# A two-layer hybrid trunk on one core: attention exponentials turned by VectorE and transfers, mixer transfers moved to GpSimd's queue, and fewer small matmuls for norms

## The chip, the cores and the metric

The kernel runs on one core of one Trainium2 chip. The core has five engines with an instruction queue each: TensorE (PE in the profile; PEld is its weight load), VectorE (DVE), ScalarE (ACT), GpSimd (POOL) and SyncE (SP). SP, ACT and POOL can also issue transfers, which 16 DMA engines carry out. The metric is device time in microseconds of one launch, lower is better.

## The reference, cut to what matters

One sequence of 256 tokens with 2048 features goes through two layers; each layer is a mixer and then a gated feed-forward block with a short convolution, all with a norm ahead and a residual around. Everything is float32.

```python
h = rms_norm(x, mix_norm[0])                       # layer 0, mixer A/B
u, v, q, f, i, g = split(h @ w_in)                 # 6 blocks of 1024 columns
u, v = gelu(u), gelu(v)
v = rms_norm(v per head)                           # A: 8 heads of 128
y_a = u * (causal_w @ v + b)                       # chunks of 128 tokens
log_f = logaddexp(log(lb), log1p(-lb) + log_sigmoid(f)); k = (1 - lb) * sigmoid(-f)
o = gated linear recurrence of q, k, i, log_f      # B: 8 heads of 128, linear in q
y_b = rms_norm(o per head, gain) * silu(g)
x = x + concat(y_a, y_b) @ w_out
x = x + conv_ffn(rms_norm(x, ffn_norm[0]))
h = rms_norm(x, mix_norm[1])                       # layer 1, mixer C
q, k, v, g, f = split(h @ w_in); q, k = rms_norm(q), rms_norm(k)   # 16 heads of 128
c = cumsum(log_sigmoid(f + b_f))                   # one number per head and token
p = softmax(causal(q @ k.T * scale + c[t] - c[s]))
x = x + ((p @ v) * sigmoid(g)) @ w_out
x = x + conv_ffn(rms_norm(x, ffn_norm[1]))
```

## The kernel before, in words

**Weights.** Every projection streams its weights from HBM in chunks of 512 KB (L181, on SP's queue). ScalarE rounds a chunk to the matmul's format (`wh`, L175) and VectorE takes the rest (`wl`, L176); activations are split the same way. A product is then three matmuls (activation high times `wh`, high times `wl`, low times `wh`), each 128x128 by 512, at L292 to L294 (`project_tok`) and L311 to L313 (`project_four`). A chunk gives twelve of these. `w` has four buffers, `wh` and `wl` three.

**Steps.** All other work is written as generators. Each chunk begins with a `tick()`: every generator in flight (at most `depth[0]`) runs to its next `yield`, and its instructions thus stand in the program ahead of that chunk's. `LAG`, `WAIT`, `PACE` are counts of such steps. A scheduler then orders each engine's instructions by priority (the order of the program) and readiness; `held(r, "wh")` or `held(r, "wl")` says that an instruction may not come ahead of the last weight half written so far, and `tied` does that for matmuls.

**Turning.** Projections give tokens on partitions where features are wanted. `transposed` does this in two moves: `blocks` (L324) transposes 32x32 blocks on VectorE, and `moves` (L331) sends 16 transfers of 32 KB from tile to tile, dealt out to SP and POOL in turn. `add_four` (L462 to L474) does it for the residual after an output projection; half of its transfers go out a step later for two of the four quarters.

**Norms.** `Norm` adds up squares of x in `acc`. `finish_tok` (L434) sums over partitions with matmuls two columns wide and gives `Rt`, the reciprocal root with tokens on partitions; `finish` (L445) sums with a 128x128 matrix of ones and gives `R`, with tokens along the row on every partition. `rsq` (L389 to L394) is the reciprocal root: a multiply-add, logarithm and exponential on ScalarE, and three VectorE operations.

**Mixer A/B.** `q` of each head is taken from PSUM by `fold` (L337, L338) and multiplied by `R` (L802, L803). `hgrn(h)` is the recurrence of one head: a small product (L681) for the diagonal, seven levels of halving with VectorE and ScalarE, small matmuls (L721), and the output (L743 to L745) in a bank of PSUM, of which there are two. ScalarE squares it there (L749), `rsq` follows, and two scaled copies (L753) write it out. `gated(j)` multiplies four heads with silu of the gate, turns them and splits them into `yb`; `spatial(j)` does the A half and gives `ya`. `values` needs `Rt` with its second half of tokens reversed, `Rr`, made by a matmul with a reversed identity (L594). The output projection (`stretch`) takes `yb` first, then `ya`.

**Mixer C.** `forget` computes the 16 forget logits with x itself (L901), so `sums` multiplies by `R`, makes the running sum `fc` and sends it through DRAM (`cd`, L928) to all partitions (`cb`, L934), on POOL's queue. The q, k, v columns come in four groups of four heads, 24 chunks a group; q and k are normed by head and turned. `attend(h)` runs for two heads at a time during the next group's chunks: scores (L954, L955), bias and mask (L958 to L962, reading `cb`), maximum (L968), exponentials, three transposes of 128x128 on TensorE (L977), a copy out of PSUM (L980), the product with v (L984 to L986) and a scaled copy (L988). `gate(q)` multiplies with sigmoid of the gate once all heads are done, turns, and splits for the output projection.

Of the kernel before, what the change touches and what calls it, by code (L numbers as in the profile page):

```python
# [15 lines left out]
P = 128  # L16
S = 256
# [9 lines left out]
FORGET = 4  # L27
WAIT = 4
# [25 lines left out]
def tile_trunk(ctx: ExitStack, tc: tile.TileContext, x, pp_d, cst_d, mlev_d, msk_d,  # L54
# [262 lines left out]
    def transposed(src, tmp, dst, queues=(nc.sync, nc.gpsimd)):  # L317

        blocks(src, tmp)
        moves(tmp, dst, queues)  # L320
# [6 lines left out]
    def moves(tmp, dst, queues=(nc.sync, nc.gpsimd), rows=range(4)):  # L327
        n = 2 * BLK
        for a in rows:
# [4 lines left out]

    def fold(ps):
        t = tp.tile([P, S], F32, tag="ev", name=nm("ev"), bufs=3)
        SC.activation(t, ps[:, S:2 * S], AF.Copy)  # L337
        V.tensor_tensor(t, ps[:, 0:S], t, ALU.add)  # L338
        return t

    def project_norm(wsrc, acts, R, out=None, run=2):
        t = fold(project(wsrc, acts, run=run))
        if out is None:
            out = t
        V.tensor_tensor(out, t, R, ALU.mult)
        return out
# [53 lines left out]
    class Norm:  # L400
# [42 lines left out]
        def finish(self, tok=False):  # L443
            ps = bank()
            PE.matmul(ps[:, 0:S], ones, self.acc, start=True, stop=True)  # L445
            R = cp.tile([P, S], F32, tag="R", name=nm("R"), bufs=2)
            rsq(R, ps[:, 0:S], D)
            if not tok:
                return R
            for _ in self.finish_tok():  # L450
                pass
            return R, self.Rt

# [6 lines left out]
    def add_four(q, ps, z, tmp, dst, nxt, halves=1):  # L460
# [25 lines left out]
    def mixer_ab(norm):  # L486
# [11 lines left out]
        gv, late = [], []  # L498

        def finish():  # L500
            for k in range(KT):
                norm.feed_square(k)
                if k % 2:
                    yield
            late.extend(norm.finish(tok=True))

        for g, ps in enumerate(project_first(w_v, norm, lambda: queue.append(finish()))):
# [5 lines left out]
            else:  # L513
                drain()
                R, Rt = late
# [77 lines left out]
        ps = bank()  # L593
        PE.matmul(ps[:, 0:2], cst[:, K_REV:K_REV + P], Rt, start=True, stop=True)  # L594
        Rr = hp.tile([P, LANE], F32, tag="Rr", name="Rr")[:, 0:2]
        V.tensor_copy(Rr[:, 0:1], Rt[:, 0:1])
        V.tensor_copy(Rr[:, 1:2], ps[:, 1:2])
# [21 lines left out]

        queue.append(mixes())  # L620
        lf, kq = [], []

        def gates(j, z):

            for _ in range(LAG):
                yield
# [15 lines left out]
        for j in range(2):  # L642
# [5 lines left out]
            transposed(lambda T: z[:, T * 512:(T + 1) * 512], tmp, t.rearrange("p (m t) -> p m t", m=4))  # L648
# [4 lines left out]
        itoks, left, os_ = [], [NH], []  # L653

# [12 lines left out]
        def hgrn(h):  # L667
# [78 lines left out]
            so = hp.tile([P, LANE], F32, tag="so", name=nm("so"), bufs=2)[:, 0:2]  # L746
            ot = hp.tile([P, P], F32, tag="ot", name=nm("ot"), bufs=1)
            for T in range(2):
                SC.activation(ot, op[:, T * P:(T + 1) * P], AF.Square,  # L749
                              accum_out=so[:, T:T + 1])  # L750
            rsq(so, so, P)
            for T in range(2):
                SC.activation(os_[h // 4][:, T, d0:d0 + P], op[:, T * P:(T + 1) * P], AF.Copy,  # L753
                              scale=so[:, T:T + 1])
# [13 lines left out]
        def gated(j):  # L768
# [17 lines left out]
            moves(tmp, t.rearrange("p (m t) -> p m t", m=4))  # L786
            for _ in range(LAG - 1):
                yield
# [5 lines left out]
        for h in range(NH):  # L794
# [16 lines left out]
        def spatial(j, z):  # L811
            for _ in range(LAG):
                yield
# [487 lines left out]
```

## Time and profile before

| what | value |
|---|---|
| runs | 2288.85, 2288.69, 2287.63 us; median 2288.69 |
| span of the profiled execution | 2287.3 us; the median of the runs is 1.4 us more, which is what lies around the span and the spread |
| granted TensorE clock | 1.000 |
| TensorE busy | 2280.8 us |
| VectorE, ScalarE, GpSimd busy | 1559.8, 1309.6, 361.2 us |
| mixer A/B, first feed-forward, mixer C, second feed-forward | about 0 to 407, 407 to 1126, 1126 to 1592, 1592 to 2287 us |

The page of the profile has busy times, the span in 40 slices, the DMA queues, the chain of work that ended last, the costliest groups and the DMA issues. A row of a timeline is: start, duration, engine, line, operation, output from input, shapes, count, and in brackets the idle time of the engine ahead of it and what ended it. A row of groups is: line, engine, operation, tiles, shapes, count, then busy time and mean ns of one, then idle time ahead of it. A row of waits is: who waited, for whom, total, times, longest. A row of one line's instructions gives the shortest, middle and longest duration in ns, and the first and last start. A row of windows gives the stretch, its length, then for each engine busy time and instructions, the granted clock, the DMA engines' share and GB/s.

### The profile page before, as it was taken

The numbers are of one execution on the slowest core, as the hardware profiler recorded it, in microseconds if no ns is written. First come the engines' busy times: TensorE is split into PE (matmuls) and PEld (weight loads), VectorE is DVE, ScalarE is ACT, GpSimd is POOL, SyncE is SP. The second block draws the span as 40 slices with busy tenths as digits, with TensorE's granted clock in tenths as the row PEclk, the third lists the DMA queues.
The fourth block names the chain that finished last, engine by engine and source line by source line (L and its number), as shares of the span: only waits on it lengthen the run. The fifth ranks groups of instructions, "written<-read, shape, count | busy, mean of one in ns | idle before, by whom it ended". The sixth has DMA issues, their size and how long they took to land.

```text
span 2287.3 us, 32261 instructions
## 1 busy us (share of the span) xinstructions
PE 2280.8 (100%) x10832; PEld 1893.5 (83%) x10832; DVE 1559.8 (68%) x2309; ACT 1309.6 (57%) x1980; POOL 361.2 (16%) x662
## 2 busy tenths in 40 slices
PE   9999999999999999999999999999999999999999
PEld 8888888888888888888888888888888888888887
DVE  7788767777467656766875675767776476657766
ACT  7677756666456445654565555655665465456642
POOL 0121221212012002111111111211211012012102
PEclk9999999999999999999999999999999999999999
DMA  8655767778667667776666655777777677667765
GB/s 288 195 169 160 215 199 235 238 216 234 193 208 221 206 201 213 220 213 186 213 227 203 194 177 181 220 224 242 225 217 218 195 216 210 209 205 216 223 204 174
DMA packets 489415, 480.45 MB, mean 210 GB/s; under 512 B 114112, under 2 KB 457168, under 8 KB 489120
## 3 DMA queue, kind: packets, MB, share of 16 engines
q1 hardware_dynamic: 467040, 453.54, 64.2%
q0 software_dynamic: 20480, 22.50, 4.3%
q10 hardware_dynamic: 1728, 2.35, 0.3%
q8 instruction: 85, 1.39, 0.3%
q14 instruction: 82, 0.67, 0.1%
HBM read 435.24 MB, written 2.11 MB: 191 GB/s over the span
## 4 chain that ended last, share of the span: by engine, by line
PE 97%; DVE 2%; ACT 1%; issue 0%; SPq 0%; DMA 0%; DVEq 0%; ACTq 0%
PE pm L311 26%; PE pm L312 26%; PE pm L313 26%; PE pm L292 4%; PE pm L294 4%; PE pm L293 4%; PE pm L193 1%; PE pm L266 1%; PE pm L217 1%; DVE wl L176 0%; PE pm L269 0%; ACT wh L175 0%; DVE kq L701 0%; PE px L955 0%; SPq L331 0%
## 5 line engine op out<-in xcount | busy, mean ns | idle before, releaser
L176 DVE TENSOR_TENSOR wl<-w,wh 128x1024 fp32r<-128x1024 f32 (+1 forms) x820 | 996.9, 1219 | 637.0 <-ACT wh L175 629.3
L175 ACT ACTIVATE wh<-w 128x1024 fp32r<-128x1024 f32 (+1 forms) x820 | 862.5, 1054 | 786.0 <-PE pm L313 552.3
L311 PE MATMUL pm<-wh,a 128*128 128x512 f32 x1728 | 674.4, 390 | 0.0
L312 PE MATMUL pm<-wl,a 128*128 128x512 f32 x1728 | 672.5, 389 | 0.0
L313 PE MATMUL pm<-wh,a 128*128 128x512 f32 x1728 | 672.5, 389 | 0.0
L331 POOL DMA_DIRECT2D zt<-tmp x413 | 223.5, 549 | 1201.6 <-DVE tmp L324 1089.8
L313 PEld LDWEIGHTS pm<-wh,a 128*128 128x128 f32 x1728 | 324.4, 188 | 67.4
L312 PEld LDWEIGHTS pm<-wl,a 128*128 128x128 f32 x1728 | 324.4, 188 | 67.3 <-DVE wl L176 0.5
L311 PEld LDWEIGHTS pm<-wh,a 128*128 128x128 f32 x1728 | 324.4, 188 | 67.1
L311 PE MATMUL pm<-wh,hid 128*128 128x512 f32 x688 | 267.6, 389 | 0.0
L312 PE MATMUL pm<-wl,hid 128*128 128x512 f32 x688 | 267.6, 389 | 0.0
L313 PE MATMUL pm<-wh,hid 128*128 128x512 f32 x688 | 267.6, 389 | 0.0
L331 POOL DMA_DIRECT2D turn<-tmp x160 | 86.7, 550 | 504.5 <-DVE tmp L324 256.7
L292 PE MATMUL pm<-wh,a 128*128 128x512 f32 x416 | 165.2, 397 | 0.0
L294 PE MATMUL pm<-wh,a 128*128 128x512 f32 x416 | 162.1, 390 | 0.0
L293 PE MATMUL pm<-wl,a 128*128 128x512 f32 x416 | 162.0, 389 | 0.0
L311 PEld LDWEIGHTS pm<-wh,hid 128*128 128x128 f32 x688 | 129.2, 188 | 26.9
L313 PEld LDWEIGHTS pm<-wh,hid 128*128 128x128 f32 x688 | 129.2, 188 | 26.8
L312 PEld LDWEIGHTS pm<-wl,hid 128*128 128x128 f32 x688 | 129.2, 188 | 26.7
L1105 ACT ACTIVATE conv<-zt,pp 128x256 f32<-128x256 f32 x176 | 95.9, 589 | 26.1 <-DMA zt<-tmp 22.2
L324 DVE STREAM_TRANSPOSE tmp<-z 128x512 f32<-128x512 f32 x120 | 83.4, 704 | 18.9 <-ACT z L1091 18.4
L294 PEld LDWEIGHTS pm<-wh,a 128*128 128x128 f32 x416 | 78.1, 188 | 16.6
(244 smaller groups left out, 2075.6 us busy)
## 6 DMA issues: line engine op xcount, KB each, us to landing
w<-in_w_up SPq DMA_DIRECT2D x352, 512.0 KB, 4.4
w<-in_w_dn SPq DMA_DIRECT2D x176, 512.0 KB, 4.5
w<-in_w_cqkv SPq DMA_DIRECT2D x96, 512.0 KB, 4.3
w<-in_w_abo SPq DMA_DIRECT2D x32, 512.0 KB, 4.6
w<-in_w_cg SPq DMA_DIRECT2D x32, 512.0 KB, 4.3
w<-in_w_co SPq DMA_DIRECT2D x32, 512.0 KB, 4.3
zt<-tmp SPq DMA_DIRECT2D x414, 32.0 KB, 2.7
zt<-tmp POOLq DMA_DIRECT2D x413, 32.0 KB, 2.5
```

The costliest lines, as they stand in the source:

```text
L175: r = deep["wh"] = SC.activation(wh, w, AF.Copy)
L176: deep["wl"] = V.tensor_tensor(wl, w, wh.bitcast(F32), ALU.subtract)
L193: PE.matmul(ps[g][T], a[:, o + T * P:o + (T + 1) * P], t[:, i * 512:(i + 1) * 512], start=k + i + j == 0, stop=k + i == KT - 1 and j == 2)
L292: PE.matmul(ps[T], ah, h, start=k + i == 0, stop=False)
L293: PE.matmul(ps[T], ah, l, start=False, stop=False)
L294: deep["last"] = PE.matmul(ps[T], al, h, start=False, stop=k + i == KT - 1)
L311: PE.matmul(ps[T], ah, h, start=not begun and k + i == ks[0], stop=False)
L312: PE.matmul(ps[T], ah, l, start=False, stop=False)
L313: deep["mm"] = deep["last"] = PE.matmul(ps[T], al, h, start=False, stop=not more and k + i == ks[-1] + 1)
L324: V.transpose(tmp.rearrange("p (b m i t) -> p b m i t", b=4, m=4, t=2)[:, :, :, :, T], src(T).rearrange("p (m b j) -> p b m j", m=4, b=4))
L331: queues[(a + b) % len(queues)].dma_start(dst[BLK * b:BLK * (b + 1), :, a * n:(a + 1) * n], tmp[BLK * a:BLK * (a + 1), b * 4 * n:(b + 1) * ...
L1105: held(SC.activation(c, z, AF.Identity, bias=pp[:, cb:cb + 1], scale=w(2)))
```

## The change

Six things change, none in the feed-forward blocks.

1. `attend` takes two heads at once. Exponentials of both lie in one tile of six 128x128 blocks; VectorE transposes their 32x32 blocks (two instructions of 128x384) and 16 transfers on POOL put the blocks in place. The transposes on TensorE and the copy out of PSUM go. The products stand six steps behind the last of the transfers' steps; a pair starts at least `PAIR` = 5 steps after the one ahead. While the gate's weights stream, three generators may be in flight.
2. All of the mixers' `moves` go to POOL alone (`ONE`), except the last set of each mixer's gate or residual (`TWO`); the readers' `LAG` grows by one step, and `add_four` no longer splits its transfers.
3. `hgrn` writes its output raw by one copy; squares are taken from the copy, scaled by `Rt`, and after every fourth head one `rsq` and two 128x512 products norm four heads. `q` is no longer multiplied by `R`: the recurrence is linear in q, so its norm is folded into the output's factor.
4. `finish` and its ones-by-`acc` matmul go from both mixers. `sums` gets its norm from four matmuls with 32 columns of ones, 64 tokens each, into four strips of 32 partitions.
5. `Rr` is made by VectorE transposes and copies in `mirror`.
6. `yB` in mixer C is filled by place.

```diff
+PAIR = 5
...
+    ONE, TWO = (nc.gpsimd,), (nc.sync, nc.gpsimd)
...
-        def finish(self, tok=False):
-            ps = bank()
-            PE.matmul(ps[:, 0:S], ones, self.acc, start=True, stop=True)
-            R = cp.tile([P, S], F32, tag="R", name=nm("R"), bufs=2)
-            rsq(R, ps[:, 0:S], D)
...
-        moves(tmp, dst, rows=range(4 // halves))
+        moves(tmp, dst, ONE if q < 3 else TWO)
 
         def rest():
-            if halves == 2:
-                yield
-                moves(tmp, dst, rows=range(2, 4))
-            for _ in range(LAG - 2 * (q == 3)):
+            for _ in range(LAG + 1 - 3 * (q == 3)):
                 yield
...
-        ps = bank()
-        PE.matmul(ps[:, 0:2], cst[:, K_REV:K_REV + P], Rt, start=True, stop=True)
+        def mirror():
+            yield
+            held(V.tensor_copy(ra, Rt[:, 1:2].to_broadcast([P, BLK])), "wl")
+            V.tensor_copy(Rr[:, 0:1], Rt[:, 0:1])
+            V.transpose(rb, ra)
+            V.transpose(ra, view(rb, BLK - 1, (-1, BLK)))
+            for a in range(4):
+                V.tensor_copy(Rr[BLK * (3 - a):BLK * (4 - a), 1:2], ra[BLK * a:BLK * (a + 1), 0:1])
...
         def gates(j, z):
-            for _ in range(LAG):
+            for _ in range(LAG + 1):
...
-            so = hp.tile([P, LANE], F32, tag="so", name=nm("so"), bufs=2)[:, 0:2]
+            o = os_[h // 4]
+            SC.activation(o[:, :, d0:d0 + P], op[:, 0:S].rearrange("p (t d) -> p t d", t=2), AF.Copy)
+            so = sos[:, h // 4]
             for T in range(2):
-                SC.activation(ot, op[:, T * P:(T + 1) * P], AF.Square,
-                              accum_out=so[:, T:T + 1])
-            rsq(so, so, P)
-            for T in range(2):
-                SC.activation(os_[h // 4][:, T, d0:d0 + P], op[:, T * P:(T + 1) * P], AF.Copy,
-                              scale=so[:, T:T + 1])
+                SC.activation(ot, o[:, T, d0:d0 + P], AF.Square, scale=Rt[:, T:T + 1],
+                              accum_out=so[:, T, h % 4:h % 4 + 1])
+            if h % 4 == 3:
+                yield
+                rsq(so, so, P)
+                V.tensor_tensor(so, so, Rt.unsqueeze(2).to_broadcast([P, 2, 4]), ALU.mult)
+                for T in range(2):
+                    o4 = o[:, T].rearrange("p (h d) -> p h d", d=P)
+                    held(V.tensor_tensor(o4, o4, so[:, T].unsqueeze(2).to_broadcast([P, 4, P]), ALU.mult), "wl")
...
-            z = fold(project(w_q[h], A))
-            V.tensor_tensor(kq[h][:, 2], z[:, 0:P], R[:, 0:P], ALU.mult)
-            V.tensor_tensor(back(kq[h][:, 1]), z[:, P:S], R[:, P:S], ALU.mult)
+            ps = project(w_q[h], A)
+            z = tp.tile([P, S], F32, tag="ev", name=nm("ev"), bufs=3)
+            SC.activation(z, ps[:, S:2 * S], AF.Copy)
+            V.tensor_tensor(kq[h][:, 2], ps[:, 0:P], z[:, 0:P], ALU.add)
+            V.tensor_tensor(back(kq[h][:, 1]), ps[:, P:S], z[:, P:S], ALU.add)
...
+            pr = bank()
+            for g in range(4):
+                PE.matmul(pr[BLK * g:BLK * (g + 1), 0:LANE], ones[:, 0:BLK], norm.acc[:, LANE * g:LANE * (g + 1)],
+                          start=True, stop=True)
...
+            rsq(Rq, pr[:, 0:LANE], D)
+            for g in range(4):
+                SC.activation(R[:, LANE * g:LANE * (g + 1)], Rq[BLK * g:BLK * g + CH], AF.Copy)
...
+        def attend(hs, q, k, v, o):
+            while steps[0] < turn[0]:
+                yield
+            turn[0] = steps[0] + PAIR
...
+            tmp = hp.tile([P, 6 * P], F32, tag="ptmp", name=nm("ptmp"), bufs=1)
+            for i, sms in enumerate(sums):
+                V.reciprocal(sms, sms)
+                t = V.transpose(tmp.rearrange("p (b m i) -> p b m i", b=4, m=6)[:, :, 3 * i:3 * i + 3],
+                                sc[:, 3 * i:3 * i + 3].rearrange("p m (b j) -> p b m j", b=4))
+                if i == 0:
+                    held(t, "wl")
+            yield
+            n = 6 * BLK
+            pt = hp.tile([P, 6, P], F32, tag="pt", name=nm("pt"), bufs=2)
+            for a in range(4):
+                for b in range(4):
+                    nc.gpsimd.dma_start(pt[BLK * b:BLK * (b + 1), :, BLK * a:BLK * (a + 1)],
+                                        tmp[BLK * a:BLK * (a + 1), b * n:(b + 1) * n]
+                                        .rearrange("p (m r) -> p m r", m=6))
+                if a == 1:
+                    yield
+            for _ in range(LAG - 1):
+                yield
...
-            queue.extend(attend(h, *qkv, os_[g]) for h in range(4 * g, 4 * g + 4))
+            queue.extend(attend((h, h + 1), *qkv, os_[g]) for h in range(4 * g, 4 * g + 4, 2))
 
         room = []
+        depth[0] = 3
...
-            moves(tmp, heads(t))
-            for _ in range(LAG - 2 * (q == 3)):
+            moves(tmp, heads(t), ONE if q < 3 else TWO)
+            for _ in range(LAG + 1 - 3 * (q == 3)):
                 yield
```

More of the change, by code (lines that the diff above doesn't have):

```diff
@@ L325, in blocks, with moves @@
                         src(T).rearrange("p (m b j) -> p b m j", m=4, b=4))
-    def moves(tmp, dst, queues=(nc.sync, nc.gpsimd), rows=range(4)):
+    def moves(tmp, dst, queues=TWO):
         n = 2 * BLK
-        for a in rows:
+        for a in range(4):
             for b in range(4):
@@ L514, in mixer_ab @@
                 drain()
[L515 removed]
+                Rt = norm.Rt
                 last = ps
@@ L973, in attend @@
             yield
             yield
-            pps = bank()
-            for b in range(3):
-                r = PE.transpose(pps[:, b * P:(b + 1) * P], sc[:, b], ident)
-                tc.add_manual_dep(r.ins, last.ins.name, order, reason="in a row")
-            pt = hp.tile([P, 3 * P], F32, tag="pt", name=nm("pt"), bufs=2)
-            SC.activation(pt, pps[:, 0:3 * P], AF.Copy)
-            yield
-            op = bank()
-            v0, v1 = (v[:, T, d0:d0 + P] for T in range(2))
-            PE.matmul(op[:, 0:P], pt[:, 0:P], v0, start=True, stop=True)
```

141 lines of the change are left out of this document (72 added, 69 removed).

## The prediction

> **What bounds the kernel now.** I read the page first (busy time, slices, chain), then TensorE's waits, then single stretches of TensorE's timeline where the change takes instructions away.
>
> ```profile
> span 2287.3 us, 32261 instructions
> PE 2280.8 (100%) x10832; PEld 1893.5 (83%) x10832; DVE 1559.8 (68%) x2309; ACT 1309.6 (57%) x1980; POOL 361.2 (16%) x662
> PEclk9999999999999999999999999999999999999999
> PE 97%; DVE 2%; ACT 1%; issue 0%; SPq 0%; DMA 0%; DVEq 0%; ACTq 0%
> ```
> ```profile
> PE px L681 <- ACT o L753: 1.1, 1, 1.1
> ...
> PE pm L312 <- DVE wl L176: 0.6, 1, 0.6
> ```
>
> TensorE is busy 2280.8 of 2287.3 us, the chain that ended last is 97% TensorE, and its waits for another engine, behind the one at the very start, are two. The clock is not held back. So time comes off in only two ways: fewer TensorE cycles, or one of these waits (1.1 and 0.6 us). Everything else can only hide, or make TensorE wait. That a busy TensorE is at its rate I take from its steps:
>
> ```profile
> 1176.16 0.39 PE L292 MATMUL pm<-wh,a 128*128 128x512 f32 x1
> ...
> 1176.61 0.39 PE L294 MATMUL pm<-wh,a 128*128 128x512 f32 x1
> 1176.84 0.81 PE L977 MATMUL px<-cst,sc 128*128 128x128 f32 x6
> 1177.41 0.47 PE L292 MATMUL pm<-wh,a 128*128 128x512 f32 x1
> 1177.73 0.39 PE L293 MATMUL pm<-wl,a 128*128 128x512 f32 x1
> ```
>
> A 512-wide matmul takes 0.39 us but the next starts 0.225 us later ((1176.61 - 1176.16) / 2). Starts, not durations, are the cost; a chunk of weights (12 such matmuls, one step of the generators) is 2.72 us.
>
> **The change, part by part.** *Transposes of the exponentials.* From L294 at 1176.61 to L293 at 1177.73 are 1.12 us where two steps would be 0.45, so the six transposes of two heads cost 0.67 us. Eight pairs: 5.4 us off TensorE.
>
> *Norm matmuls and the reversed Rt.*
>
> ```profile
> 49.44 0.59 PE L445 MATMUL px<-acc,ones 128*128 128x256 f32 x2
> 49.87 0.50 PE L434 MATMUL px<-ones,acc 128*128 128x2 f32 x4
> ...
> 53.29 0.39 PE L312 MATMUL pm<-wl,a 128*128 128x512 f32 x1
> 53.52 0.28 PE L594 MATMUL px<-Rt,cst 128*128 128x2 f32 x2
> ...
> 53.98 0.39 PE L311 MATMUL pm<-wh,a 128*128 128x512 f32 x1
> ...
> 185.99 0.43 PE L681 MATMUL px<-kq 128*32 128x64 f32 x16 [1.10 <-ACT o L753]
> ```
>
> The full-width sum (L445) takes 49.44 to 49.87, 0.43 us, in each mixer: 0.86 off. Mixer C gets four 32-column ones of 64 elements instead. L681 has that shape: 16 records (eight matmuls, two records each) in 0.43, so four are 0.21; with no overlap they would be 0.43 (the moved columns are the same as L445's). I take 0.21, since L681 also writes different 32-row strips. L594: 53.29 to 53.98 is 0.69 for two steps of 0.45, so 0.24 off; its eight small VectorE copies are not waited for until L763, four heads later. Sum: 5.4 + 0.86 - 0.21 + 0.24 = 6.3 us.
>
> *Recurrence.* The last row shows the 1.1 us wait: L681 needs a PSUM bank that the previous head's output holds until two squares, a reciprocal root and two scaled copies are through. Afterwards one copy frees it; I count the 1.1 as gone. The stage also gets lighter:
>
> ```profile
> 110.00:190.00 80.00, 78.82 (x747) 66.39 (x746) 69.99 (x170) 59.74 (x171) 19.87 (x28) 1.00 0.57 172
> ...
> L338 DVE TENSOR_TENSOR ev<-pm,ev 128x256 f32<-128x256 f32 x8 | 3.3, 414 | 0.0
> ...
> L778 DVE TENSOR_TENSOR gz<-gz,o 128x512 f32<-128x512 f32 x4 | 2.7, 679 | 3.1 <-ACT gz L98 3.1
> ```
>
> VectorE is busy 70 of 80 us here, the fullest stretch. It loses L338 (3.3 us; L802 and L803 stay as adds) and the small operations of six of the eight reciprocal roots, which I leave uncounted, and gains four 128x512 products (2.7 as L778): at least 0.6 us lighter, so no new wait is expected from it. What is late next: the norm of heads 3 and 7 waits one step more, so the gated outputs come one to two steps (5.4 us) later; they have room:
>
> ```profile
> 277.00 0.75 ACT L376 ACTIVATE yb<-o,pp 128x256 fp32r<-128x256 f32 x1
> ...
> L311 PE MATMUL pm<-wh,yb x64: 389/389/389, 292.2 to 368.6; 128*128 128x512 f32 x64
> ...
> 294.36 4.32 POOL L331 DMA_DIRECT2D turn<-tmp  x8 [17.43 <-issue]
> ...
> 301.48 0.41 ACT L98 ACTIVATE zu<-turn 128x256 f32<-128x256 f32 x1
> ```
>
> The last yb starts at 277; TensorE's first use of any is at 292.2. The second u transfer is tighter: 16 on POOL instead of 8 end at 303.2, plus landing (below) 305.6, while L98 moves from 301.48 to one step later, 304.2: 1.4 us short. It is ScalarE that would wait, with products begun ahead as cover; taken at nothing, up to 1.4.
>
> *Transfers off SP.* The 0.6 us wait is for a weight half late at the output projection. The chain of waits leads to SP, which issued eight transfers and only then that weight:
>
> ```profile
> 338.54 1.95 SPq L331
> ...
> 343.81 4.01 DMA w<-in_w_abo
> ```
>
> Those eight go to POOL, and I count the 0.6 as gone. POOL now issues all of a set:
>
> ```profile
> L331 POOL DMA_DIRECT2D turn<-tmp x160: 548/548/665, 74.3 to 1570.6; - x160
> DMA to landing us min/median/max: 1.7/2.4/6.7
> ```
>
> A set takes 16 x 0.55 = 8.8 us instead of 4.4; readers come one step (2.72) later, so it is up to 1.7 us short wherever nothing else waits. Weight halves are made two chunks ahead (5.44 us); less L175 (1.06) and L176 (1.22) that leaves about 3 us of cover. Taken at nothing. The last set of each mixer keeps both queues and its step count.
>
> *Attention in pairs.* VectorE gets 16 transposes of 384 (0.704 x 384/512 = 0.53 us each, by L324 below), ScalarE loses the 16 copies of the transposes out of PSUM; 128 transfers join POOL. POOL in all: +(72 + 112 + 128) x 0.55 = +171 us on 361 (nine sets and fourteen sets of eight leave SP, eight pairs have 16 each), still mostly idle. Their price hangs on whether a pair's blocks land before its product, which TensorE takes in program order.
>
> ```profile
> L324 DVE STREAM_TRANSPOSE tmp<-z 128x512 f32<-128x512 f32 x120 | 83.4, 704 | 18.9 <-ACT z L1091 18.4 <-ACT z L462 0.4
> 1170.04 0.38 PE L954 MATMUL px<-qk 128*128 128x128 f32 x2
> ...
> 1171.16 0.58 PE L292 MATMUL pm<-wh,a 128*128 128x512 f32 x1
> ...
> 1176.12 0.19 ACT L98 ACTIVATION_READ_ACCUMULATOR sc<-sc,mxs 128x1 f32 x1
> ...
> 1187.04 0.38 PE L954 MATMUL px<-qk 128*128 128x128 f32 x2
> ...
> 1203.13 4.37 POOL L331 DMA_DIRECT2D turn<-tmp  x8 [42.51 <-DVE tmp L324]
> ```
>
> A pair's scores cost TensorE 1.3 us (1170.04 to 1171.16, and the step after it is a long one); its product sends as many columns, 768, and is taken as the same. Scores to exponentials: 1170.04 to 1176.31, 6.3 us. Second pair: its scores were at 1187.04, now 2.0 earlier (transposes 0.67 gone, first pair's product 1.3 moved behind) at 1185.0; exponentials 1191.3, transposes and reciprocals 1192.7, 16 transfers 1201.5, landed 1203.9. Its product stands nine chunks after the scores: 1185.0 + 1.3 + 24.5 + 1.3 (first pair's product) = 1212.1. Slack 8.2 us; the first pair has the same. q's set, 1203.13 before, comes at about 1202 and just misses them. Price nothing; bound under the rivals.
>
> *The forget sums.* The tightest place.
>
> ```profile
> 1152.15 4.33 POOL L331 DMA_DIRECT2D turn<-tmp  x8 [6.65 <-DVE f L920]
> 1156.47 0.51 POOL L928 DMA_DIRECT2D cd<-fc  x1
> 1158.44 2.18 POOL L934 DMA_DIRECT2D cb<-cd  x4 [1.46 <-DMA cd<-fc]
> DMA to landing us min/median/max: 9.1/11.1/14.1
> 1170.89 0.35 DVE L958 SCALAR_TENSOR_TENSOR sc<-px,ct,cb 128x128 f32<-128x128 f32 x1 [0.63 <-PE px L955]
> ...
> 1173.39 1.22 DVE L176 TENSOR_TENSOR wl<-w,wh 128x1024 fp32r<-128x1024 f32 x1
> ```
>
> cd goes out right behind k's transfers on POOL; with 16 of them that is 4.4 us later, so cb starts at about 1162.9 and lands (9.1 to 14.1) between 1172.0 and 1177.0, where L958 stood ready at 1170.9: VectorE blocked 1.1 to 6.1 us, L176 behind it. That half ends at 1174.6 and feeds the chunk whose second matmul is at 1177.73 (1177.06 without transposes): cover 2.4. So TensorE waits 0 to 3.7 us; at the median 11.1, 3.1 less 2.4. I take 1.0, a little over that, for the weights that share the queue with cb.
>
> Sum: -6.3 - 1.1 - 0.6 + 1.0 = -7.0. The profiled span 2287.3 becomes 2280.3; the median of the runs is 1.4 above that span (launch and spread), so **2281.7 us**, 0.3% faster. The measurement can tell 0.2%, 4.6 us, from no change.
>
> **A rule that speaks against it.** The POOL rows above are 548 to 665 ns beside a VectorE that is two thirds busy: no stretching. The Trainium skill, "SBUF — State Buffer", section "A bandwidth-pool intuition that's wrong (but worth ruling out)", says that a transfer issued by GpSimd waits for descriptors while VectorE holds a shared port in a two-port mode, about 620 ns alone becoming 3100. By it, an estimate, 16 transfers would take 50 us, 41 past the slack, at eight pairs over 300 us slower; by the rows nothing. The trace does not agree for the operations that this kernel runs on VectorE.
>
> **The rivals.** (1) *TensorE waits at the pairs' products*, the case on the slow side. If q's 16 transfers go ahead of the second pair's on POOL (they stand earlier in the program), those start at 1202 + 8.8 = 1210.8 and land at 1222.0, 9.9 us after the product's place; half of them, 5.5. Three groups have it: 16 to 30 us, less 7.0: 2298 to 2312, mid 2304. It decides once POOL is more than 8.2 us late. For it: the two sets miss each other by half a microsecond. Against: the four cb issues stand far apart in the program and went out together, so queues follow readiness, and the pair is ready ten microseconds before q. 0.13. (2) *Covers wear out*: late landings (up to 1.7 at some twenty sets, 3.7 at cb, 1.4 at u) let through 3 to 7 us in all: 2284 to 2289, mid 2286. For it: margins of a microsecond at single chunks, as at cb; against: 3 us of cover everywhere else. 0.18. (3) *Transfers on POOL run slower as they pile up* (landing 6.7 and issue 0.665 always): 16 x 0.117 + 4.3 = 6.2, under 8.2, so the pairs hold, but cb and the gates lose some 4 each: +10, 2292. 0.05. This is the mechanism of the rule in the Trainium skill ("SBUF — State Buffer") as far as the rows bear it out. That rule in full has 0.02. (4) *The wait at L681 stays* (the bank's copy queues behind a weight half): 2282.8; within the forecast.
>
> **How the numbers follow.** Forecast with its own range 2280.4 (no new wait at all, 2287.3 - 8.0, runs 1.1 under the median) to 2284.1: 0.62. Faster 0.62 + 0.04 of rival 2 = 0.66. Same: the rest of 2 (0.14) and 3 (0.05) = 0.19. Slower: 1 and the rule = 0.15. The range runs from 2280.0 to 2290.0, over the forecast and rival 2, 0.80.
>
> **What would show it.** TensorE busy about 2273.5 us; no L977 transposes; no wait at L681 over 0.3; POOL about 530 us; chunks of 2.72 through mixer C with 1.3 us per pair's scores and products. Wrong if TensorE's waits name a landing of the turned exponentials, or a weight half behind the first use of cb, or a wait in the gates, where two sets now follow on POOL within one or two steps.

## The result

The changed kernel takes 2283.92 us (median of 21 runs, 2281.74 to 2286.11) against 2287.66 us before (21 runs, 2286.77 to 2289.09): a ratio of 0.9982, 95% interval 0.9977 to 0.9988, or 3.7 us less. The forecast was 2281.7 us, 7.0 less. The way was right and the time lies in the range (2280.0 to 2290.0), but only about half of the gain came.

The page of the changed kernel, its span, busy times and the shares of the chain that ended last:

```profile
span 2281.0 us, 32087 instructions
...
PE 2273.9 (100%) x10786; PEld 1887.8 (83%) x10786; DVE 1561.2 (68%) x2301; ACT 1301.8 (57%) x1946; POOL 528.8 (23%) x974
...
PE 96%; DMA 2%; DVE 1%; POOL 1%; issue 0%; ACT 0%; SPq 0%; ACTq 0%; DVEq 0%; POOLq 0%
```

TensorE lost 6.9 us of busy time (2280.8 to 2273.9) and still sets the span. All of TensorE's waits of the changed kernel:

```profile
PE warm L145 <- DVE ones L85: 1.1, 1, 1.1
PE pm L218 <- ACT wh L176: 0.8, 1, 0.8
PE pm L313 <- DVE wl L177: 0.8, 1, 0.8
PE pm L294 <- DVE wl L177: 0.7, 1, 0.7
```

The two waits of before (1.1 at L681, 0.6 at L312 for `wl`) are gone, and two new ones on weight halves are here (L313 in a feed-forward, L294 in mixer C); the 0.8 at L218 is at the start, behind the load of x.

Where the time went is read from the first matmul of each `finish_tok`, which opens a stage. Before (its first, at 49.87, stands in the prediction), and then after, in TensorE's timelines:

```profile
407.32 0.52 PE L434 MATMUL px<-ones,acc 128*128 128x2 f32 x4
...
1125.97 0.50 PE L434 MATMUL px<-ones,acc 128*128 128x2 f32 x4
...
1591.82 0.52 PE L434 MATMUL px<-ones,acc 128*128 128x2 f32 x4
```
```profile
50.05 0.50 PE L424 MATMUL px<-ones,acc 128*128 128x2 f32 x4
...
404.79 0.52 PE L424 MATMUL px<-ones,acc 128*128 128x2 f32 x4
...
1124.51 0.50 PE L424 MATMUL px<-ones,acc 128*128 128x2 f32 x4
...
1585.36 0.52 PE L424 MATMUL px<-ones,acc 128*128 128x2 f32 x4
```

The differences of these rows, and of the same rows of the kernels below (all one profiled execution each), give the length of each stage; the last ends with the span.

| kernel | mixer A/B | first feed-forward | mixer C | second feed-forward |
|---|---|---|---|---|
| before | 357.45 | 718.65 | 465.85 | 695.5 |
| after | 354.74 | 719.72 | 460.85 | 695.6 |
| the same again (k6) | 355.08 | 719.85 | 459.88 | 695.7 |
| second buffer (k1) | 354.77 | 719.99 | 461.58 | 695.6 |
| group 0 on both queues (k2) | 354.76 | 719.88 | 459.88 | 696.4 |
| second buffer, group 0 on both queues (k5) | 354.77 | 719.56 | 461.46 | 696.2 |
| both queues, added steps (k3) | 356.19 | 718.80 | 463.23 | 695.7 |
| attention of before (k4) | 355.05 | 719.77 | 466.47 | 697.0 |
| pairs seven steps apart (k7) | 355.21 | 719.85 | 463.57 | 695.6 |
| norms only (k8) | 355.40 | 718.72 | 466.36 | 695.6 |
| six memsets (k9) | 355.03 | 719.77 | 461.81 | 695.6 |
| transfers of before (k10) | 355.20 | 718.67 | 462.72 | 695.5 |
| transfers of before, second buffer (k11) | 355.48 | 718.60 | 461.01 | 695.5 |
| second buffer, six memsets (k12) | 354.80 | 719.80 | 460.97 | 695.6 |

So in the profiled executions the change is worth -2.7 in A/B (forecast -1.9: 0.24, 1.1 and 0.6; the 0.43 of the first L445 lies ahead of the stage's first row), -5.0 in C (forecast -4.6: 5.4, 0.43 less 0.21, and 1.0 back) and +1.1 in the first feed-forward, which the change does not touch (forecast 0). After and k6 are the same kernel and differ by up to 1.0 us in a stage (mixer C), so smaller differences in the mixers are not read. The last column holds the tail, too: from the start of the last matmul to the end of the span are 4.1 us in after, but 4.8 in k2 and 5.4 in k4.

The spans differ by 6.3, near the 7.0 forecast. The medians differ by 3.7 only, because the two profiled executions are not the usual ones. Before's span was 2287.3, while the 87 executions of before that ran beside the experiments had median spans of 2286.6, 2285.7 and 2286.1. Their times lie 1.9 us above their spans, so the median of 2287.66 stands for a span of about 2285.8, and the trace of before is some 1.5 us long. The trace of after (2282.78 us, span 2281.0) is 1.1 us short of the median span of its runs, 2282.1. Then 6.3 - 1.5 - 1.1 = 3.7. So some 3.2 of the 6.9 us that TensorE lost do not reach the time. After's trace names 1.5 us of new waits behind the start; where the rest lies in the other executions is not shown.

### The profile page after: what moved, and what is told of

It reads as the page before. It is cut to its first block, busy times and chain, and to the rows that moved or that the text cites. A ratio compares the mean times of both kernels' runs of the same rounds, so it can differ in the third digit from the quotient of the medians.

```text
span 2281.0 us, 32087 instructions
## 1 busy us (share of the span) xinstructions
PE 2273.9 (100%) x10786; PEld 1887.8 (83%) x10786; DVE 1561.2 (68%) x2301; ACT 1301.8 (57%) x1946; POOL 528.8 (23%) x974
## 4 chain that ended last, share of the span: by engine, by line
PE 96%; DMA 2%; DVE 1%; POOL 1%; issue 0%; ACT 0%; SPq 0%; ACTq 0%; DVEq 0%; POOLq 0%
PE pm L312 26%; PE pm L313 26%; PE pm L314 26%; PE pm L293 4%; PE pm L294 4%; PE pm L295 4%; PE pm L267 2%; PE pm L194 1%; PE pm L270 1%; DMA turn<-tmp 0%; DMA pt<-ptmp 0%; POOL turn L334 0%; DMA cb<-cd 0%; DMA x<-in_x 0%; PE pm L218 0%
## 5 line engine op out<-in xcount | busy, mean ns | idle before, releaser
L177 DVE TENSOR_TENSOR wl<-w,wh 128x1024 fp32r<-128x1024 f32 (+1 forms) x820 | 995.8, 1218 | 624.2 <-ACT wh L176 615.7
L312 PE MATMUL pm<-wh,a 128*128 128x512 f32 x1728 | 674.7, 390 | 0.0
L313 PE MATMUL pm<-wl,a 128*128 128x512 f32 x1728 | 672.9, 389 | 0.0
L314 PEld LDWEIGHTS pm<-wh,a 128*128 128x128 f32 x1728 | 324.5, 188 | 67.4
L312 PEld LDWEIGHTS pm<-wh,a 128*128 128x128 f32 x1728 | 324.5, 188 | 67.1
L313 PEld LDWEIGHTS pm<-wl,a 128*128 128x128 f32 x1728 | 324.6, 188 | 66.7
L313 PE MATMUL pm<-wl,hid 128*128 128x512 f32 x688 | 268.0, 389 | 0.8 <-DVE wl L177 0.8
L312 PE MATMUL pm<-wh,hid 128*128 128x512 f32 x688 | 267.9, 389 | 0.0
L334 POOL DMA_DIRECT2D turn<-tmp x304 | 165.0, 550 | 267.5 <-DVE tmp L327 145.5
L294 PE MATMUL pm<-wl,a 128*128 128x512 f32 x416 | 162.3, 390 | 0.7 <-DVE wl L177 0.7
L313 PEld LDWEIGHTS pm<-wl,hid 128*128 128x128 f32 x688 | 129.2, 188 | 27.9 <-DVE wl L177 1.2
L312 PEld LDWEIGHTS pm<-wh,hid 128*128 128x128 f32 x688 | 129.2, 188 | 26.7
L294 PEld LDWEIGHTS pm<-wl,a 128*128 128x128 f32 x416 | 78.2, 188 | 16.8 <-DVE wl L177 1.1
```

What stands on the lines that cost most here:

```text
L177: deep["wl"] = V.tensor_tensor(wl, w, wh.bitcast(F32), ALU.subtract)
L294: PE.matmul(ps[T], ah, l, start=False, stop=False)
L312: PE.matmul(ps[T], ah, h, start=not begun and k + i == ks[0], stop=False)
L313: PE.matmul(ps[T], ah, l, start=False, stop=False)
L314: deep["mm"] = deep["last"] = PE.matmul(ps[T], al, h, start=False, stop=not more and k + i == ks[-1] + 1)
L334: queues[(a + b) % len(queues)].dma_start(dst[BLK * b:BLK * (b + 1), :, a * n:(a + 1) * n], tmp[BLK * a:BLK * (a + 1), b * 4 * n:(b + 1) * ...
```

## The experiments

The ratios below are to the kernel before on the same chip, with 95% intervals; and "11 runs" counts executions.

### Is the gain that of the pairs? Attention undone, and the norms alone

First the changed kernel with `attend` of before, one head each and transposes on TensorE (k4):

```diff
-            queue.extend(attend((h, h + 1), *qkv, os_[g]) for h in range(4 * g, 4 * g + 4, 2))
+            queue.extend(attend(h, *qkv, os_[g]) for h in range(4 * g, 4 * g + 4))
...
-        depth[0] = 3
```

> The changed kernel with the attention of before (three transposes a head on TensorE, copy out of PSUM, heads one by one, two in flight). TensorE busy rises by 5.4 to about 2279.3. If the pairs bring no wait of their own the median is 5.4 above the changed kernel, 2289.3, above the kernel before. Theory A: the pairs cost 1.5 to 3 of their 5.4, so it is 2286.3 to 2287.8. If it is under 2285 the pairs gain nothing at all.

Then only norms, recurrence and mirror, with attention, transfers and step counts of before (k8):

```diff
-    ONE, TWO = (nc.gpsimd,), (nc.sync, nc.gpsimd)
+    ONE = TWO = (nc.sync, nc.gpsimd)
...
-            for _ in range(LAG + 1):
+            for _ in range(LAG):
```

> Only the norm matmuls, the reversed Rt and the recurrence are changed; attention, transfers and step counts are those of before. By the forecast it is 0.9 us less TensorE work and the 1.1 us wait, 2.0 under the kernel before. The changed kernel with the old attention came out 1.5 above the kernel before; if this one is 1 to 2 below, moving the transfers to POOL cost 2.5 to 3.5 of it and was no gain. If this one is above too, the cost lies in the norms or the recurrence.

k4 took 2290.0 us, ratio 1.0006 [0.9997, 1.0015]: without the pairs nothing of the gain is left. By the two ratios that is 5.5 us more than the changed kernel, which is the figure expected if the pairs bring no wait of their own (5.4) and not theory A's; but 1.4 us of it may be the longer tail of k4's table row. k8 took 2286.95 us, 0.9998 [0.9989, 1.0007]: the norms and the recurrence alone are worth nothing that can be measured (0.7 us, where 2.0 were expected). TensorE's busy time, k4 and then k8:

```profile
PE 2280.1 (100%) x10834; PEld 1892.2 (83%) x10834; DVE 1555.4 (68%) x2285; ACT 1308.9 (57%) x1962; POOL 458.2 (20%) x846
```
```profile
PE 2279.9 (100%) x10834; PEld 1892.5 (83%) x10834; DVE 1556.9 (68%) x2285; ACT 1308.3 (57%) x1962; POOL 359.9 (16%) x662
```

From 2280.8 before, the norms take off 0.7 (k4) to 0.9 (k8) (forecast 0.43 + 0.43 - 0.21 + 0.24 = 0.89); from there to after the pairs take off 6.0 to 6.2 (forecast 5.4). Kernels with the same matmuls as after read 2273.5 (k11) to 2275.8 (k3), so the tenths are not exact, but both terms of TensorE stand. By stage, k8 has A/B at 355.40, 2.05 less than before.

### Do the pairs' transfers land in time?

The slack at the second pair was forecast as 8.2 us. The transfers of the turned exponentials in the changed kernel, by their line (durations in ns, first and last start; then the landing):

```profile
L1001 POOL DMA_DIRECT2D pt<-ptmp x128: 565/567/597, 1178.1 to 1413.2; - x128
...
DMA to landing us min/median/max: 1.7/4.0/5.7
```

POOL's timeline of the first group's two pairs, and then TensorE's at the second pair's product:

```profile
1178.07 6.88 POOL L1001 DMA_DIRECT2D pt<-ptmp  x12 [11.09 <-DVE ptmp L992]
1185.12 0.56 POOL L1001 DMA_DIRECT2D pt<-ptmp  x1 [0.17 <-issue]
1186.90 1.68 POOL L1001 DMA_DIRECT2D pt<-ptmp  x3 [1.22 <-DMA pt<-ptmp]
1195.21 4.46 POOL L1001 DMA_DIRECT2D pt<-ptmp  x8 [6.62 <-DVE ptmp L992]
1201.33 4.47 POOL L1001 DMA_DIRECT2D pt<-ptmp  x8 [1.66 <-issue]
```
```profile
1211.40 0.38 PE L1013 MATMUL px<-v,pt 128*128 128x128 f32 x2
```

The first pair's set takes 10.5 us (1178.07 to 1188.58), not 16 x 0.55 = 8.8: behind the twelfth and the thirteenth transfer POOL stops, at the end until an earlier one has landed. The second pair's last transfer is issued at 1205.24. The same view for it alone; the landing counts from the start of the issue:

```profile
L1001 POOL DMA_DIRECT2D pt<-ptmp x1: 565/565/565, 1205.2 to 1205.2; - x1
...
DMA to landing us min/median/max: 2.5/2.5/2.5
```

So the blocks are there at about 1207.8, and the product is at 1211.40: 3.6 us of slack in place of 8.2, the smallest of the eight pairs (the others have 4.8 to 6.9). The set began 2.5 us later than forecast (1195.21 for 1192.7), took 1.8 longer (10.6 for 8.8), landed 0.4 sooner behind its last issue, and the product stood 0.7 earlier. No wait at L1013 is among TensorE's waits. To see the price when the slack is used up, pairs were held seven steps apart instead of five (k7):

```diff
-PAIR = 5
+PAIR = 7
```

> One block buffer as in the changed kernel, but pairs start seven steps apart instead of five, 5.4 us more for the pair ahead to land. Theory A: no wait at L992 and the same gain as two buffers, 2281.2 to 2282.3. If the gain of two buffers came from the order of instructions or from chance, this stays at 2283.5 to 2284.3. The gate starts two steps later; that may cost up to 1 us in either case.

It took 2285.28 us, 0.9989 [0.9980, 0.9998], not the 2281.2 to 2282.3 of theory A. VectorE's wait at L992 (the next section) is gone, but TensorE has a new one. Its longest wait, and POOL at the first group's second pair, where 0.4 of the 2.8 us fall:

```profile
PE px L1013 <- DMA pt<-ptmp: 2.8, 3, 1.7
```
```profile
1197.06 6.50 POOL L334 DMA_DIRECT2D turn<-tmp  x12 [10.21 <-DVE tmp L327]
1206.24 2.17 POOL L334 DMA_DIRECT2D turn<-tmp  x4 [2.69 <-issue]
1208.40 3.37 POOL L1001 DMA_DIRECT2D pt<-ptmp  x6
1212.22 5.59 POOL L1001 DMA_DIRECT2D pt<-ptmp  x10 [0.45 <-DMA turn<-tmp]
```

This is rival (1): q's set goes first, the pair's transfers behind it, and the product waits. It is real, and `PAIR` = 5 keeps it away; but it costs 2.8 us over three places, not the 16 to 30 that I gave it: in k7 the pair starts two steps later, and by the code its product stands two steps later too.

### The single buffer of turned blocks

Where the pairs do cost something is one engine earlier. VectorE's waits for transfers in the changed kernel, then VectorE's and TensorE's timelines at the longest:

```profile
DVE ptmp L992 <- DMA pt<-ptmp: 5.5, 4, 3.7
...
DVE sc L974 <- DMA cb<-cd: 1.6, 1, 1.6
```
```profile
1188.25 0.15 DVE L991 RECIPROCAL sms<-sms 128x2 f32<-128x2 f32 x1
1192.08 0.58 DVE L992 STREAM_TRANSPOSE ptmp<-sc 128x384 f32<-128x384 f32 x1 [3.68 <-DMA pt<-ptmp]
1192.58 1.18 DVE L177 TENSOR_TENSOR wl<-w,wh 128x1024 fp32r<-128x1024 f32 x1
```
```profile
1193.82 0.50 PE L294 MATMUL pm<-wl,a 128*128 128x512 f32 x1 [0.67 <-DVE wl L177]
```

`ptmp` has one buffer. The second pair's transpose waits 3.68 us until the first pair's blocks have left, the weight half L177 is queued behind it, and TensorE waits 0.67 for that half. The prediction has no such wait. Four kernels bear on it: a second buffer (k1), group 0's q and k sets on both queues (k2), both together (k5), and the changed kernel once more (k6).

```diff
-            tmp = hp.tile([P, 6 * P], F32, tag="ptmp", name=nm("ptmp"), bufs=1)
+            tmp = hp.tile([P, 6 * P], F32, tag="ptmp", name=nm("ptmp"), bufs=2)
```

> The block buffer ptmp of the turned exponentials gets two buffers instead of one; nothing else. TensorE lost 6.9 us of busy time (2280.8 to 2273.9) but the median fell 3.7, so some 3 us of new waits are to be found. Theory A (VectorE stands at L992 until the pair ahead has landed, 3.7 us once in the profile, and late weight halves follow): the wait at L992 is gone and the median falls by 1 to 2 us under the changed kernel, to 2282 to 2283. Theory B (cb lands late, L974) and theory C (sets on POOL alone land late everywhere): no change, 2283.5 to 2284.3. In every theory TensorE stays busy 2273 to 2274.5.

```diff
-                    transposed(lambda T: z[:, T], flat(piece("tmp", 2)), heads(t), ONE)
+                    transposed(lambda T: z[:, T], flat(piece("tmp", 2)), heads(t), ONE if g else TWO)
```

> Only the first group's q and k sets go back to SP and POOL in turn, so cd leaves POOL some 4 us earlier. Theory B: cb lands before its first reader (no wait at L974, 1.6 us in the changed kernel's profile), median 0.5 to 2 us under the changed kernel, 2282 to 2283.4. Theories A and C: 2283.5 to 2284.3.

> Two block buffers, and the first group's q and k sets on both queues. Theory A alone: like two block buffers, 2281.5, spans under 2281. With theory B too: another 0.5 to 1 less, 2280.5 to 2281. Never under 2279.5, where TensorE's busy time of 2273.9 and what lies around it end.

> The changed kernel once more, for its spread and a second profile. Its spans lay in two groups, 2280.0 to 2281.9 and 2282.1 to 2284.3 us. Theory A (VectorE stands at the single block buffer, longer in some executions): a profile of the upper group shows more than 5.5 us of VectorE waits at L992 and weight halves late behind them, in mixer C. If a profile of the upper group loses its time outside mixer C, theory A falls.

| kernel | median us | runs from, to | ratio |
|---|---|---|---|
| second buffer (k1) | 2281.5 | 2281.07, 2282.81 (6) | 0.9972 [0.9960, 0.9983] |
| group 0 on both queues (k2) | 2283.08 | 11 runs | 0.9980 [0.9971, 0.9989] |
| both (k5) | 2283.11 | 11 runs | 0.9981 [0.9972, 0.9989] |
| the same again (k6) | 2282.99 | 2281.28, 2285.77 (11) | 0.9981 [0.9972, 0.9990] |

The second buffer takes the wait at L992 away (no row of it in k1 and k5), but the four intervals overlap: with the sets on POOL the buffer's worth lies between nothing (k5 against k6) and some 2 us (k1 against k6 by their ratios; they ran on different chips, k1 in six runs), and these runs do not settle it. k5 misses the 2281.5 us that theory A gave it. The profile of k6 is of its shorter group (span 2279.9), so the expectation about the upper group stays untested. VectorE waits 3.8 us at L992 there and TensorE for no weight half in mixer C, so this wait does not reach TensorE in every execution. The wait for `cb` is absent in k2, but with the same edit it is there in k5 (2.4 us); k2 moves the time by nothing that can be seen.

### The sets' move to POOL

The changed kernel with all sets on both queues again, its added steps kept (k3), and with the steps, too, as before (k10); then k10 with the second buffer (k11).

```diff
-    ONE, TWO = (nc.gpsimd,), (nc.sync, nc.gpsimd)
+    ONE = TWO = (nc.sync, nc.gpsimd)
```

> All sets of the mixers go to SP and POOL in turn again, with the changed kernel's step counts (one step more than before); the pairs' transfers stay on POOL. Theory C: late landings on POOL cost 1 to 3 us, the median falls to 2281 to 2283. If SP's weight queue was what paid before (as forecast, 0.6 us at the output projection), it rises by 0.5 to 1.5, to 2284.5 to 2285.5. Theories A and B: A unchanged; B falls as in the run with only the first group.

> Pairs and norms as in the changed kernel, but every mixer set on both queues and with the step counts of before (the whole second part undone). Theory A: moving the sets costs the 2 us that two kernels with the old attention differed by (2.1 us): 2281.5 to 2282 us, ratio 0.997 to 0.9975. Theory B: with the pairs it costs nothing, as in the kernel with both queues and the added steps (0.9982): 2283.5 to 2284.5 us, with the wait of the output projection (0.6 us at about 350 us) back.

> The kernel with every set on both queues and the step counts of before, pairs and norms kept, and a second buffer for the turned blocks. If the buffer's hold on VectorE (3.7 us waited at L992, 0.7 us of it passed on to TensorE) is worth its microsecond here as it was in the changed kernel (0.9982 to 0.9972), this is 1 to 2 us shorter than the same kernel with one buffer; if POOL with half as many transfers ahead of the pairs frees the buffer in time anyway, it is equal to it within 0.5 us.

k3 took 2284.08 us, 0.9982 [0.9973, 0.9990]; k10 2284.06 us, 0.9983 [0.9974, 0.9992]; k11 2281.92 us, 0.9974 [0.9963, 0.9984]. So theory B of k10: with the pairs, moving the sets to POOL is worth nothing that can be seen. The wait of the output projection, which theory B expects back, is not in k10's trace; it is in k3's (0.8 at 348.65) and, smaller, in k8's and k11's (0.2 and 0.3), and in none of the nine kernels with the sets of A/B on POOL. By stage the move gains 0.1 to 0.5 in A/B (355.20 to 355.08 in k6 and 354.74 in after) and loses 1.1 in the first feed-forward (718.67 to 719.72). And here the buffer does show: all eight runs of k11 (2281.57 to 2282.93) lie at or below the fastest of the eleven of k10 (2282.93 to 2285.33), 2.1 us between the medians. TensorE's waits on weight halves in k10, and then in k11:

```profile
PE pm L294 <- DVE wl L177: 2.1, 2, 1.4
```
```profile
PE pm L294 <- DVE wl L177: 0.8, 1, 0.8
```

The 1.4 us of k10 are at 1192.8, the place of the fence above; in k11 they are gone and the 0.8 at 1306.9 stays. Mixer C goes from 462.72 to 461.01. So the single buffer's price is shown there: a wait on VectorE that passes on to TensorE by way of a weight half. The traces show 1.3 to 1.7 of the 2.1 us.

k10 also corrects my reading of the forget sums. I put `cb`'s lateness on POOL, whose 16 transfers stand ahead of `cd`. With both queues the wait is there as well. VectorE's wait in k10; POOL's issue of `cd` and `cb` there; then the last step of the norm's root and the running sum that they wait for, in before and in k10:

```profile
DVE sc L977 <- DMA cb<-cd: 3.0, 1, 3.0
```
```profile
1156.67 0.51 POOL L932 DMA_DIRECT2D cd<-fc  x1 [4.41 <-DVE fc L930]
1161.78 2.19 POOL L938 DMA_DIRECT2D cb<-cd  x4 [4.60 <-DMA cd<-fc]
```
```profile
1147.73 0.40 DVE L394 SCALAR_TENSOR_TENSOR R<-rt,R 128x256 f32<-128x256 f32 x1
...
1154.73 0.68 DVE L926 TENSOR_TENSOR_SCAN fc<-on,f 16x256 f32<-16x256 f32 x1
```
```profile
1150.05 0.23 DVE L384 SCALAR_TENSOR_TENSOR Rq<-rt,Rq 128x64 f32<-128x64 f32 x1
...
1155.70 0.68 DVE L930 TENSOR_TENSOR_SCAN fc<-on,f 16x256 f32<-16x256 f32 x1
```

Counted from the start of mixer C (1125.97 before; 1122.74 in k10), `fc` comes at 28.8 before and at 33.0 in k10: 4.2 us later. The last step of the norm's root starts 21.8 us into the stage before and 27.3 in k10, and four small copies (`Rf`, from the new matmuls' strips) follow it. POOL sat idle 4.41 us ahead of `cd`. And `cd` took 1.7 us to land before and 4.8 in k10 (4.1 after). In after `cb` goes out 7.8 us later than before (1164.8 against 1158.44, each from the start of its mixer C), where I forecast 4.4: 4.2 from the sum, 2.4 from the landing of `cd`, and 1.2 from POOL's queue (2.3 us from the end of `fc` at 1158.14 to `cd` at 1160.44, against 1.1 before).

### The first feed-forward

It is 0.8 to 1.4 us longer in every kernel with the sets of A/B on POOL alone (719.56 to 719.99, against 718.60 to 718.80 in before, k3, k8, k10 and k11). k4 is one of them and has no pairs, so the sets do it. In the changed kernel, POOL's timeline, ScalarE's and TensorE's:

```profile
989.29 2.71 POOL L334 DMA_DIRECT2D zt<-tmp  x5 [17.43 <-DVE tmp L327]
994.23 1.63 POOL L334 DMA_DIRECT2D zt<-tmp  x3 [2.23 <-issue]
```
```profile
1000.79 1.09 ACT L1136 ACTIVATE conv<-zt,pp 128x256 f32<-128x256 f32 x2 [4.01 <-DMA zt<-tmp]
```
```profile
1010.29 0.50 PE L313 MATMUL pm<-wl,hid 128*128 128x512 f32 x1 [0.79 <-DVE wl L177]
```

Five transfers of a set go out, then POOL pauses for 2.23 us with nothing to wait for, and the convolution stands 4.01 us on ScalarE; the weight halves behind it are late and TensorE waits. In k10 the set goes in one piece (8 transfers from 988.66) and the convolution starts at 996.05. I took the pause for one of POOL's own instruction stream, and moved that stream by six small instructions (k9), and by these and the second buffer (k12):

```diff
+    for n in range(6):
+        nc.gpsimd.memset(cp.tile([P, LANE], F32, tag="pad", name=nm("pad"), bufs=1)[:, n:n + 1], 0.0)
```

> The changed kernel with six one-element memsets on POOL at the very start; nothing else is touched. Theory: the first feed-forward is 1.1 us longer in every kernel with the mixers' sets on POOL alone (719.6 to 720.0 us, against 718.6 to 718.8 in the kernels that keep both queues) because a pause of 2.2 us in POOL's own instruction stream has moved into a set of eight there (five transfers at 989.3, the other three only at 994.2). Six more instructions on POOL end the pause before that set: first feed-forward 718.7 us, no wait of L313 near 1010 us, ratio to before 0.9977 (1.1 us less than the changed kernel's 0.9982). Rival: the 0.8 us wait there comes from the order of the weights' loads: it stays at about 1010 us, the stage stays at 719.7 us and the ratio at 0.998.

> The changed kernel with a second buffer for the turned blocks and the six memsets on POOL at the start. If the two effects are separate places they add: 1 us from the buffer and 1.1 us from the first feed-forward, 2280.5 to 2281.5 us, ratio 0.9968 to 0.9972, TensorE's waits behind the first one under 0.5 us together. If the pause on POOL only moves to another set that matters, 2281.5 to 2283 us and a wait of 0.5 us or more at another place.

POOL's timeline in k9:

```profile
988.91 2.72 POOL L336 DMA_DIRECT2D zt<-tmp  x5 [17.41 <-DVE tmp L329]
993.85 1.63 POOL L336 DMA_DIRECT2D zt<-tmp  x3 [2.22 <-issue]
```

The pause stays behind the same fifth transfer, the stage at 719.77, TensorE's wait at 1010.01 with 0.88 us. My theory of the instructions fell. What the pauses do keep is a count of transfers: in before and in k10 POOL issues 113 transfers ahead of the first pause and 106 to the next, in after, k9 and k12 113, 106 and again 106, and the third falls into this set. The sets moved to POOL use up the count sooner. Why it pauses there is not shown, and a kernel that moves the third pause by transfers was not run. That the pause is what lengthens the stage is thus argued: from the rows above, and because all nine kernels with a pause in this set wait 0.67 to 0.95 us at about 1010 and none of the other five does. k9 took 2282.39 us, 0.9975 [0.9965, 0.9985], its ratio as hoped but with none of the mechanism; k12 2282.49 us, 0.9975 [0.9965, 0.9984]. k12 waits at 1010 as well. It is also k9 with a second buffer, on the same chip, and no shorter. TensorE's waits in mixer C, k9 and then k12:

```profile
1194.41 0.50 PE L296 MATMUL pm<-wl,a 128*128 128x512 f32 x1 [1.34 <-DVE wl L179]
```
```profile
1476.76 0.50 PE L315 MATMUL pm<-wl,yc 128*128 128x512 f32 x1 [0.76 <-DVE wl L179]
```

The buffer takes the wait of k9 away, and another one appears at the output projection of mixer C. k1 and k5 have it there, too (1.1 and 1.0 us in all); no kernel with one buffer has it, nor k11. So in these traces part of the buffer's gain is lost again further on when the sets are on POOL; what makes that weight half late is not shown.

The shortest kernels are k1, k11, k9 and k12, 0.9972 to 0.9975; their intervals do not tell them apart. Only k11 against k10 was a clear step.

## Why the prediction was right, and where it was off

The time lies at the upper end of the forecast's own range (2280.4 to 2284.1), 2.2 us above the forecast: 0.7 in the profiled span (2281.0 for 2280.3), 1.1 because the usual execution of after is longer than the profiled one, and 0.4 from span to time. That the span came so near is partly luck. The first feed-forward (1.1) and the stretch ahead of the first row (0.6: it grew by 0.18 instead of losing 0.43) are worse than forecast, A/B (0.8) and C (0.4) better.

- **TensorE's cycles (-6.3).** Right, and a little short: -6.9 of busy time, 0.9 from norms and mirror and 6.0 from the pairs. No row of transposes is left.
- **The waits of before (-1.1 and -0.6).** Gone from the trace, and mixer A/B is 2.7 shorter. But both were read from one execution, whose span was 0.7 to 1.6 us above the medians of before's other executions. Norms only (k8) has A/B shorter by 2.05 in its trace and 0.7 us in its median (2286.95 against 2287.64). I priced what one execution showed as if each run paid it. That the missing microsecond is just these two waits is argued: no other execution of before has a trace.
- **"Weight halves ... Taken at nothing."** The step that failed. Two places were not free: the first feed-forward (+1.1, shown by stage in all kernels with the sets on POOL alone; that the pause does it is argued) and the wait for the buffer `ptmp` (0.67 in the profiled execution, 1.4 in k10). Both reach TensorE as a late `wl`, as rival (2) has it: covers that wear out. Its time, 2284 to 2289, begins just above the measured 2283.92.
- **The pairs' slack (8.2 us).** The sign held and TensorE never waited for a product, but the size was wrong: 10.6 us for 16 transfers rather than 8.8, and a pair that starts 2.5 us late behind the wait for the buffer. 3.6 us were left at the second pair.
- **The forget sums (+1.0).** Place and size of VectorE's wait held (1.6 us, inside 1.1 to 6.1), and TensorE lost nothing there. The size is luck: `cb` went out 7.8 us later rather than 4.4, mostly by the norm's root and the landing of `cd`, then landed after 9.7 us (median) rather than 11.1, and its first reader, too, stood later in the stage (46.3 us after its start rather than 44.9).
- **Rival (3) and the rule in the Trainium skill ("SBUF — State Buffer", section "A bandwidth-pool intuition that's wrong (but worth ruling out)").** The rule has a transfer from GpSimd wait while VectorE holds a shared port. By the rows above a transfer of the pairs took POOL 0.565 to 0.597 us beside a VectorE that is 68% busy, and POOL's busy time came to 528.8 us, forecast 361 + 171 = 532. No stretching shows in this trace; whether VectorE ever held the port here, no run shows. The issue did not slow, as rival (3) feared, but the landing did, for every set that POOL issues alone (median of the 32 KB transfers on POOL 4.3 us against 1.9, rows at the end), and in the changed kernel TensorE lost nothing by it at `cb` or at the gates.
- **From span to time.** I added 1.4 us to the span. Each run of after is about 1.8 us above its own span (2282.78 for 2281.0), so the execution of before that I started from was a long one: 2287.3 + 1.8 = 2289.1, an estimate, against a median of 2287.66.

## What to carry to other kernels

When work is moved from the engine that sets the time to transfers, count each tile on the new way: a producer with one buffer waits for the landing of the last transfer, and what stands behind it on that engine (here a weight half) brings the wait back to the bound engine. Credit a wait that one profiled execution shows only after comparing that execution's span with the spread of the runs. And look for the price in stages that the change leaves alone: a queue that is given more transfers stops at other places than before.

## What was not expected of the hardware

- POOL pauses 2.1 to 2.8 us, with no releaser in the profile, after its 113th transfer and, while only the block sets go, again after each 106 or 107 more. This holds in all fourteen traces, and six more instructions on POOL left the pauses behind the same transfers (994.23 in after, 993.85 in k9). A pause is free at some places: before has one at 908.77 (2.37 us) in the same stage, where ScalarE's convolution waited 4.05 us and TensorE did not.
- Sixteen transfers that POOL issues in a row are not paced by the issue alone (0.567 us each for those of 24 KB): in several sets it stops until an earlier one lands (the 1.22 us at 1186.90 after). And they land later. POOL's share of the block sets into `turn`, with the median from issue to landing: before, where each set goes out on two queues, and after, where POOL issues nearly all of them alone.

```profile
turn<-tmp POOLq DMA_DIRECT2D x160, 32.0 KB, 1.9
```
```profile
turn<-tmp POOLq DMA_DIRECT2D x304, 32.0 KB, 4.3
```

- In k10, with these sets on two queues again, they land after 2.1 us, while the pairs' sixteen, still on POOL alone, land after 4.0 as in the changed kernel.
- One small transfer to DRAM (`cd`, 16 partitions) took 1.7 us to land before and 3.5 to 4.9 in the twelve kernels of the others whose traces give it. No run here shows why.
